# Low parts of the first eight weight tiles to VectorE, the causal mask's cast to ScalarE

## The chip, the cores and the metric

The kernel runs on one NeuronCore of one Trainium2 chip. The metric is the device time of one execution in microseconds (us); the time before is the median of three runs. The engines are called by the profile's names: PE (TensorE's matmuls), PEld (its weight loads), DVE (VectorE), ACT (ScalarE), POOL (GpSimd) and SP (SyncE, which issues the weight transfers).

## What is computed

Two layers of a decoder trunk on 256 tokens of width 1024, batch 1, in float32. Each layer normalises its input, multiplies it with one combined projection, sends the columns through two attention groups and a final projection, and adds a squared-ReLU MLP. Cut to the part that matters here:

```python
for l in range(DEPTH):                       # DEPTH = 2
    h = _rms_norm(x, attn_norm[l])
    proj = h @ w_in[l]                       # 1024 -> 1720 columns
    (q_a, k_c, v_c, k_s, v_s, k_w, v_w, g_a, c_q, c_kv, k_r) = jnp.split(proj, offsets, axis=-1)
    ...                                      # sparse attention o_a and latent attention o_b, both causal
    x = x + mixed @ w_out[l]
    h = _rms_norm(x, mlp_norm[l])
    x = x + jnp.square(jax.nn.relu(h @ w_ff1[l])) @ w_ff2[l]
return _rms_norm(x, final_norm)
```

## The kernel before

**Products in three passes.** A dense product is done as three matmuls on numbers split into a high part (rounded to the type fp32r) and a low part (the rest): high times high (line 352), high activation times low weight (353), low activation times high weight (354), in `mm3`. Every weight tile is therefore split after it has landed.

**The weight stream.** `PLAN` lists the weight tiles in the order in which PE uses them; `ask(n)` keeps up to `n` tiles ahead. For a tile it issues the transfer into one of six `raw` buffers on SP's queue (line 321), and, where the tile is to be split, has ACT cast it to `whi` in two halves (line 334) and DVE or POOL subtract, `wlo = raw - whi`, in two halves (line 336). There are six buffers of `whi` and `wlo`. A tile here is "tile n", the n-th entry of `PLAN`, counted from 1. In a layer tiles 1 to 4 are the block `kcs` (two chunks of 512 columns each, so a half is one chunk), 5 to 8 the block `q` (the same), 9 to 11 `kw` (280 columns a chunk, three chunks), 12 to 15 `lat` (416 columns), 16 to 18 the latent up-projections, 19 to 26 the compression weights, which are not split, and then the output projection and the MLP.

**Who subtracts.** `lo_eng()` (line 312) gives tiles 1 and 2 of the whole run and all odd tiles to DVE, even ones to POOL. `at_w[1]` is the tile's number.

**The start.** `main` loads `x` in four quarters with the gain and tile loads in between, and four `norm` chains make the normalised activations: DVE multiplies by the gain (line 425), PE transposes (line 384), ACT casts the high part (line 393) and DVE subtracts the low part (line 394). The order of the four is half 0 of token tiles 0 and 1 (`h_191` high, `h_192` low), then half 1 of both (`h_241` high, `h_242` low). PE meanwhile runs `proj_both` for block `kcs` of layer 0: pairs of chunks, token tile 0 and then token tile 1 for each pair; chunks 4 to 7 (tiles 3 and 4) need half 1. After it PE runs block `q` from tile 5. `kcs_after` rotates the results on DVE (lines 446, 449, 451, 455) and copies the others on ACT (line 868).

**The mask.** `main` casts the causal mask from the constants `cs` into `maskb` (line 1171); `mask_for` multiplies it into the attention scores (line 652).

**What sets the order.** PE's and SP's orders are written by `Driver`, a list scheduler with ranks and estimated times that runs when the kernel is built. DVE, ACT and POOL are ordered by the framework's own scheduler at build time, each engine then executing strictly in that order; `urgent()` raises the priority of a few instructions, among them lines 393, 394 and 425.

Of the kernel before, what the change touches and what calls it, by code (L numbers as in the profile page):

```python
# [17 lines left out]
L = 2  # L18
# [87 lines left out]
def _plan():  # L106
    plan = []

    def add(chunks, per, n, split=True):
        plan.extend((min(per, chunks - a), n, split) for a in range(0, chunks, per))  # L110

    for name, (_, n) in BLOCKS.items():
        add(KC, PER_TILE[name], n)
    add(1, 1, 1024)
    add(2, 1, 768)
    add(16, 2, 512, False)
    add(16, 2, 512)
    for q in range(NQ):
        add(32, 2, 512)
    return plan  # L120


PLAN = _plan() * L
# [103 lines left out]
def trunk(ctx: ExitStack, tc: tile.TileContext, x, wst, gains, pos, cw2, cst, out):  # L227
    nc = tc.nc
# [28 lines left out]
    def load_x(t, nb):  # L257
        n = slice(nb * 512, nb * 512 + 512)
        nc.sync.dma_start(X[t][:, n], x[t * P : (t + 1) * P, n])
# [19 lines left out]
    def K(name):  # L279
        a, n = CST[name]  # L280
        return cs[:, a : a + n]
# [4 lines left out]
    maskb = const.tile([P, P], BF16, name="maskb")  # L286
# [7 lines left out]
    def warm_up(n):  # L294
        if n:
            o = PS("s")
        for _ in range(n):
            mm(o, zero, zero[:, None, :].to_broadcast([P, 4, P]), start=True, stop=True)
# [9 lines left out]
    at_w = [0, 0]  # L308
    queue = []

    def lo_eng():
        return "v" if at_w[1] <= 2 or at_w[1] % (len(PLAN) // L) % 2 == 1 else "g"

    def ask(n):

        while at_w[1] < len(PLAN) and len(queue) < n:
            k, cols, split = PLAN[at_w[1]]
            at_w[1] += 1
            m = k * cols
            r = raw_p.tile([P, 1024], F32, name="raw")  # L320
            nc.sync.dma_start(r[:, :m], wst[at_w[0] : at_w[0] + P * m].rearrange("(p n) -> p n", p=P))
            at_w[0] += P * m
            part = lambda a: [a[:, c * cols : (c + 1) * cols] for c in range(k)]
            if split:
                hi = wp.tile([P, 1024], F32R, name="whi")
                lo = wp.tile([P, 1024], F32R, name="wlo")
                eng = lo_eng()

                def cuts(n):
                    step = m // n  # L330
                    return [slice(a, a + step) for a in range(0, m, step)]

                for v in cuts(2):
                    nc.scalar.copy(hi[:, v], r[:, v])  # L334
                for v in cuts({"v": 2, "g": 2}[eng]):
                    E(eng).tensor_sub(lo[:, v], r[:, v], hi[:, v].bitcast(F32))  # L336
                queue.append(list(zip(part(hi), part(lo))))
            else:
                queue.append(part(r))

    def weights(chunks):

        while chunks:
            ask(1 + 4)
            got = queue.pop(0)
            chunks -= len(got)
            yield from got
# [62 lines left out]
    def after_x(t, a, n):  # L410

        ss = sumsq(X[t][:, a : a + n], n)
        r = sm.tile([P, 1], F32, name="mean", bufs=6)
        nc.gpsimd.tensor_scalar(r, ss, 1.0 / D, EPS if a == 0 else mean[t], op0=OP.mult, op1=OP.add)
        mean[t] = r
# [42 lines left out]
    def layer(l, hT):  # L458
# [487 lines left out]
        for ch, r in enumerate(weights(16)):  # L946
            for j in range(4):
                a, hf = divmod(j, 2)
                mm(  # L949
                    hid[32 * j : 32 * j + 32, :],  # L950
                    FT[:, a, ch].rearrange("p g b -> p (g b)"),
                    r[:, a * 256 + hf * 128 : a * 256 + hf * 128 + 128],
                    start=ch == 0,
                    stop=ch == 15,
                    tile_position=(0, 32 * j),
                )
            yield "pe", 300, 0
        dr.spawn(1, hidden_chain(hid))


# [158 lines left out]
    def begin(l, halves=()):  # L1119

        g = gain(l, "attn", halves)
        h = [None, None]
        if l == L:
            for t in range(NT):
                dr.spawn(0, finish(t, g))
        else:
            for nb in range(2):
                for t in range(NT):
                    dr.spawn(0, norm(t, nb, g, h, (l, "attn")))
        return h  # L1130
# [16 lines left out]
    def main():  # L1147
        def load_a():
            nc.sync.dma_start(idt, cst[:, :P])
            load_x(1, 0)  # L1150
            ask(2)

        def load_b():
            load_x(1, 1)
            ask(5)

        def next_x():
            load_a()
            load_x(0, 1)

        load_x(0, 0)
        h = begin(0, (next_x, load_b))
        for t in range(NT):
            for nb in range(2):
                dr.event(("x", t, (0, "attn"), nb * 512), [2000, 5000, 2600, 5500][2 * t + nb])
        for nb in range(2):
            for t in range(NT):
                after_x(t, nb * 512, 512)
        nc.sync.dma_start(cs, cst)
        nc.vector.tensor_copy(identb, ident)  # L1170
        nc.vector.tensor_copy(maskb, K("causal"))
        yield "event", ("h", 0, (0, "attn"), 0)
        warm_up(4)
        for l in range(L):
            h = yield from layer(l, h)

    dr.spawn(9, main())
    with tc.manual_schedule(engines={mybir.EngineType.PE, mybir.EngineType.SP}):
        dr.run()
# [19 lines left out]
```

## Time and profile before

| | |
|---|---|
| median of three runs | 642.43 us |
| the three runs | 642.43, 645.75, 640.5 us |
| the profiled execution, own time | 646.11 us |
| its span, first to last instruction | 644.3 us |
| PE busy / DVE / ACT / POOL | 621.4 / 420.4 / 354.6 / 300.4 us |
| mean granted clock of PE | 0.986 of full |

The profile is one execution of its own and lies above all three runs shown. Times in the rows are microseconds from the start of the span, and in a row of the timeline the first number is the start, the second the busy time of the merged instructions, "x4" their count, and the bracket the idle time of that engine just before with what ended it. Ends of matmuls are modelled; starts are what to compare.

### The profile page before, as it was taken

The page shows a single profiled execution, that of the slowest core. Times are in us where ns is not written, and L with a number is a line of the kernel's source. Part 1 is how long each engine was busy: PE and PEld are TensorE (multiplying, and loading weights), DVE is VectorE, ACT ScalarE, POOL GpSimd, SP SyncE. Part 2 cuts the span into 40 slices and gives each one's busy share as a digit, 9 for nine tenths or more (in the row PEclk, how much of TensorE's full clock was granted, in tenths as well). Part 3 has the DMA queues.
Part 4 walks back from the last instruction along what each step waited for, and adds up shares of the span by engine and source line. Part 5 has one row for each costly group of instructions (what it writes and reads, how often), then busy time and mean ns, then how long its engine had stood idle before and what let it go on. Part 6 is the DMA issues. An engine that isn't in the chain of part 4 may idle for free.

```text
span 644.3 us, 10909 instructions
## 1 busy us (share of the span) xinstructions
PE 621.4 (96%) x4099; PEld 548.3 (85%) x4099; DVE 420.4 (65%) x665; ACT 354.6 (55%) x735; POOL 300.4 (47%) x298
## 2 busy tenths in 40 slices
PE   7899899999999999999999889999999999999995
PEld 4697688889889899899888768798998998998985
DVE  4797778675656647558677866866664673764662
ACT  5566667565535546355564475765663654554551
POOL 2675404344553645445466631244544554554351
PEclk8899999999999999999999898999999999999998
DMA  8756733155555655745644665114547565565601
GB/s 306 264 175 206 236 116 100 34 198 173 185 169 191 208 182 166 226 155 186 213 126 134 211 212 199 34 66 149 177 142 220 164 200 174 193 204 176 198 1 66
DMA packets 31732, 108.48 MB, mean 168 GB/s; under 512 B 3776, under 2 KB 4416, under 8 KB 31680
## 3 DMA queue, kind: packets, MB, share of 16 engines
q1 hardware_dynamic: 31392, 107.27, 50.8%
q8 instruction: 32, 0.52, 0.3%
q10 hardware_dynamic: 288, 0.52, 0.2%
q14 instruction: 20, 0.16, 0.1%
HBM read 106.73 MB, written 1.05 MB: 167 GB/s over the span
## 4 chain that ended last, share of the span: by engine, by line
PE 85%; DVE 7%; ACT 4%; DMA 3%; issue 1%; SPq 0%; POOL 0%; POOLq 0%; ACTq 0%
PE acc L352 24%; PE acc L354 24%; PE acc L353 24%; PE tr L384 4%; DVE wlo L336 2%; PE pv L708 2%; DMA raw<-in_wst_dram 2%; PE pv L759 2%; ACT whi L334 1%; PE acc L949 1%; PE s L693 1%; DMA x<-in_x_dram 1%; PE s L746 1%; ACT p L646 1%; DVE qmT L233 1%
## 5 line engine op out<-in xcount | busy, mean ns | idle before, releaser
L336 POOL TENSOR_TENSOR wlo<-raw,whi 128x512 fp32r<-128x512 f32 (+3 forms) x178 | 245.0, 1397 | 221.2 <-ACT whi L334 220.9
L334 ACT CAST whi<-raw 128x512 fp32r<-128x512 f32 (+2 forms) x360 | 201.4, 610 | 113.6 <-PE acc L354 74.7
L336 DVE TENSOR_TENSOR wlo<-raw,whi 128x512 fp32r<-128x512 f32 (+3 forms) x182 | 170.5, 973 | 58.4 <-ACT whi L334 58.3
L352 PE MATMUL acc<-h,whi 128*128 128x256 f32 x512 | 145.3, 284 | 0.0
L354 PE MATMUL acc<-h,wlo 128*128 128x256 f32 x512 | 145.0, 283 | 0.0
L353 PE MATMUL acc<-h,whi 128*128 128x256 f32 x512 | 145.0, 283 | 0.0
L352 PE MATMUL acc<-whi,u 128*128 128x512 f32 (+1 forms) x264 | 101.5, 384 | 0.0
L353 PE MATMUL acc<-wlo,u 128*128 128x512 f32 (+1 forms) x264 | 101.2, 383 | 0.0
L354 PE MATMUL acc<-whi,u 128*128 128x512 f32 (+1 forms) x264 | 101.1, 383 | 0.0
L352 PEld LDWEIGHTS acc<-h,whi 128*128 128x128 f32 x512 | 98.3, 192 | 0.2
L353 PEld LDWEIGHTS acc<-h,whi 128*128 128x128 f32 x512 | 98.3, 192 | 0.2
L354 PEld LDWEIGHTS acc<-h,wlo 128*128 128x128 f32 x512 | 98.3, 192 | 0.0
L1057 DVE TENSOR_TENSOR sq<-relu 128x512 f32<-128x512 f32 x32 | 37.2, 1161 | 38.9 <-ACT relu L1053 38.9
L354 PEld LDWEIGHTS acc<-whi,u 128*128 128x128 f32 x264 | 49.6, 188 | 9.8
L353 PEld LDWEIGHTS acc<-wlo,u 128*128 128x128 f32 x264 | 49.7, 188 | 9.4
L352 PEld LDWEIGHTS acc<-whi,u 128*128 128x128 f32 x264 | 49.7, 188 | 9.3
L1029 DVE SCALAR_TENSOR_TENSOR x<-acc,r,x 128x512 f32<-128x512 f32 (+1 forms) x33 | 24.1, 731 | 49.0 <-PE acc L354 49.0
L1053 ACT ACTIVATE relu<-acc 128x512 f32<-128x512 f32 x32 | 19.0, 594 | 59.3 <-PE acc L354 59.3
L352 PE MATMUL acc<-whi,h 128*128 128x512 f32 (+2 forms) x112 | 41.2, 368 | 0.0
L353 PE MATMUL acc<-wlo,h 128*128 128x512 f32 (+2 forms) x112 | 40.2, 359 | 0.2 <-POOL wlo L336 0.2
L354 PE MATMUL acc<-whi,h 128*128 128x512 f32 (+2 forms) x112 | 39.9, 357 | 0.0
L646 ACT ACTIVATE p<-s,nm 128x128 f32<-128x128 f32 (+1 forms) x96 | 33.9, 430 | 7.9 <-DVE nm L640 4.0
(185 smaller groups left out, 913.3 us busy)
## 6 DMA issues: line engine op xcount, KB each, us to landing
raw<-in_wst_dram SPq DMA_DIRECT2D x178, 512.0 KB, 4.2
raw<-in_wst_dram SPq DMA_DIRECT2D x8, 416.0 KB, 3.3
raw<-in_wst_dram SPq DMA_DIRECT2D x4, 420.0 KB, 3.3
raw<-in_wst_dram SPq DMA_DIRECT2D x4, 384.0 KB, 3.1
x<-in_x_dram SPq DMA_DIRECT2D x4, 256.0 KB, 6.3
g_mix<-in_gains_dram SPq DMA_DIRECT2D x2, 512.0 KB, 5.8
g_mlp<-in_gains_dram SPq DMA_DIRECT2D x2, 512.0 KB, 5.1
g_attn<-in_gains_dram SPq DMA_DIRECT2D x2, 512.0 KB, 3.9
```

The lines of the kernel that those rows point to most:

```text
L334: nc.scalar.copy(hi[:, v], r[:, v])
L336: E(eng).tensor_sub(lo[:, v], r[:, v], hi[:, v].bitcast(F32))
L352: mm(acc, ah, wh, start=start, stop=False, **k)
L353: mm(acc, ah, wl, start=False, stop=False, **k)
L354: mm(acc, al, wh, start=False, stop=stop, **k)
L384: nc.tensor.transpose(tr[:rows, c, :], col, ident)
L646: nc.scalar.activation(p[:, k], s[:, k], AF.Exp, bias=nm[:, a : a + 1], scale=scale)
L708: mm(o[:, a, br, :], pts[a // per][:, ((a % per) * 2 + br) * nk + kt, :], V[:, kt, br, g, :], start=kt == 0, stop=kt == nk - 1)
L759: mm(o[:, r, :], pts[r // per][:, (r % per) * nk + kt, :], VM[:, kt, hb * 4 + r, :], start=kt == 0, stop=kt == nk - 1)
L1029: nc.vector.scalar_tensor_tensor(X[t][:, c], acc, scale, X[t][:, c], op0=OP.mult, op1=OP.add)
L1053: nc.scalar.activation(r, acc, AF.Relu)
L1057: nc.vector.tensor_mul(sq, r, r)
```

## The change

The subtraction `wlo = raw - whi` of tiles 4, 6 and 8 of layer 0 goes from POOL to DVE (tiles 1, 2, 3, 5 and 7 were there already). The cast of the mask goes from DVE to ACT. A statement without effect (`if True:`) shifts the line numbers behind it by one. Layer 1 is left as it is, since the tile number runs on.

```diff
     def lo_eng():
-        return "v" if at_w[1] <= 2 or at_w[1] % (len(PLAN) // L) % 2 == 1 else "g"
+        return "v" if at_w[1] <= 8 or at_w[1] % (len(PLAN) // L) % 2 == 1 else "g"
@@
-            yield "pe", 300, 0
+            if True:
+                yield "pe", 300, 0
@@
         nc.vector.tensor_copy(identb, ident)
-        nc.vector.tensor_copy(maskb, K("causal"))
+        nc.scalar.copy(maskb, K("causal"))
```

The framework orders DVE, ACT and POOL anew. On DVE, at the point in layer 0 where the low parts of half 1 are made (`h_242`, first for token tile 0, then for token tile 1) and block `kcs` of token tile 0 is rotated:

```order
 L394 TENSOR_TENSOR h_242<-tr,h_241 128x4x128
-L336 TENSOR_TENSOR wlo<-raw,whi 128x512 x2
-L1171 CAST maskb<-cs 128x128
+L336 TENSOR_TENSOR wlo<-raw,whi 128x512 x4
 L394 TENSOR_TENSOR h_242<-tr,h_241 128x4x128
-L336 TENSOR_TENSOR wlo<-raw,whi 128x512
+L336 TENSOR_TENSOR wlo<-raw,whi 128x512 x3
 L446 SCALAR_TENSOR_TENSOR ra<-s,rx,cs 128x128
 L449 SCALAR_TENSOR_TENSOR rb<-s,rx,cs 128x2x32 x2
 L336 TENSOR_TENSOR wlo<-raw,whi 128x512
+L451 TENSOR_TENSOR kd<-ra,rb 128x256
+L336 TENSOR_TENSOR wlo<-raw,whi 128x512
```

Between the two `h_242` there stand four halves (tiles 4 and 5) where two halves (tile 5) and the mask stood; behind the second there are three halves (tile 6 and the first of tile 7) where there was one, and the last three halves of tiles 7 and 8 lie between the rotations.

On POOL, behind the row scales of both token tiles, before its first halves of block `kw`:

```order
 L863 TENSOR_TENSOR rx<-mean,mhalf 128x1
 L864 TENSOR_SCALAR rx<-rx 128x1
-L336 TENSOR_TENSOR wlo<-raw,whi 128x512 x6
 L336 TENSOR_TENSOR wlo<-raw,whi 128x420 x2
 L336 TENSOR_TENSOR wlo<-raw,whi 128x416 x2
```

The six halves of tiles 4, 6 and 8 are gone; POOL's next work is tile 10.

On ACT, at the high part of half 1 of token tile 1 (the second `h_241`):

```order
 L334 CAST whi<-raw 128x512 x4
 L393 CAST h_241<-tr 128x4x128
+L1172 CAST maskb<-cs 128x128
 L334 CAST whi<-raw 128x512 x6
+L334 CAST whi<-raw 128x420 x2
```

The mask stands directly behind the high part of half 1 and ahead of the casts of tiles 6, 7 and 8; the cast of tile 9 has moved ahead of the copies of line 868. The orders of PE and SP are the same in both kernels.

## Rows read from the trace of the kernel before

**Rows 1.** The page, its head and part 1: busy us, share, count.

```profile
span 644.3 us, 10909 instructions
...
PE 621.4 (96%) x4099; PEld 548.3 (85%) x4099; DVE 420.4 (65%) x665; ACT 354.6 (55%) x735; POOL 300.4 (47%) x298
```

**Rows 2.** Stretches: length; busy PE, PEld, DVE, ACT, POOL; clock; DMA share; GB/s.

```profile
40.00:60.00 20.00, 18.73 (x123) 17.45 (x122) 18.03 (x36) 11.72 (x32) 16.73 (x25) 1.00 0.60 188
...
125.00:200.00 75.00, 75.00 (x477) 68.02 (x476) 45.73 (x60) 41.04 (x76) 36.23 (x30) 1.00 0.55 179
```

**Rows 3.** Who PE waited for, whole run: us in total, times, longest.

```profile
PE s L354 <- DVE h L394: 2.7, 1, 2.7
...
PE tr L384 <- DVE qT L530: 1.3, 1, 1.3
```

**Rows 4.** The chain that ended last, in time: start, us, what.

```profile
20.82 1.28 DVE maskb L1171
22.10 0.61 DVE h L394
...
63.12 5.27 DMA raw<-in_wst_dram
```

**Rows 5.** PE in order of time, around the wait for the last low part.

```profile
19.71 0.40 PE L353 MATMUL s<-wlo,h 128*128 128x512 f32 x1
22.76 0.80 PE L354 MATMUL s<-whi,h 128*128 128x512 f32 x1 [2.65 <-DVE h L394]
...
25.84 0.39 PE L352 MATMUL s<-whi,h 128*128 128x512 f32 x1
...
27.90 0.39 PE L352 MATMUL acc<-whi,h 128*128 128x512 f32 x1
```

**Rows 6.** DVE in order of time, 6 to 27 us.

```profile
6.55 0.22 DVE L1170 CAST identb<-idt 128x128 bf16<-128x128 f32 x1
...
10.35 2.49 DVE L336 TENSOR_TENSOR wlo<-raw,whi 128x512 fp32r<-128x512 f32 x4
...
16.79 0.69 DVE L394 TENSOR_TENSOR h<-tr,h 128x512 fp32r<-128x512 f32 x1 [1.41 <-ACT h L393]
18.34 2.55 DVE L336 TENSOR_TENSOR wlo<-raw,whi 128x512 fp32r<-128x512 f32 x2 [0.86 <-ACT whi L334]
...
22.02 0.68 DVE L394 TENSOR_TENSOR h<-tr,h 128x512 fp32r<-128x512 f32 x1
...
26.81 0.35 DVE L446 SCALAR_TENSOR_TENSOR ra<-s,rx,cs 128x128 f32<-128x128 f32 x1 [3.01 <-PE s L354]
```

**Rows 7.** DVE in order of time, window 19.5 to 19.9 alone.

```profile
19.12 1.77 DVE L336 TENSOR_TENSOR wlo<-raw,whi 128x512 fp32r<-128x512 f32 x1
```

**Rows 8.** POOL in order of time, its low parts up to tile 10.

```profile
17.36 8.82 POOL L336 TENSOR_TENSOR wlo<-raw,whi 128x512 fp32r<-128x512 f32 x6 [0.88 <-ACT whi L334]
31.25 2.49 POOL L336 TENSOR_TENSOR wlo<-raw,whi 128x420 fp32r<-128x420 f32 x2 [5.08 <-ACT whi L334]
```

**Rows 9.** ACT in order of time, 16 to 30 us.

```profile
16.65 2.18 ACT L334 CAST whi<-raw 128x512 fp32r<-128x512 f32 x4
18.73 0.58 ACT L393 CAST h<-tr 128x512 fp32r<-128x512 f32 x1
19.21 3.22 ACT L334 CAST whi<-raw 128x512 fp32r<-128x512 f32 x6
...
29.50 0.36 ACT L868 ACTIVATE V<-s,rx 128x128 f32<-128x128 f32 x1
```

**Rows 10.** Short stretches, columns as in rows 2.

```profile
22.70:25.50 2.80, 2.74 (x7) 2.17 (x8) 1.10 (x1) 0.00 (x0) 2.80 (x3) 0.50 0.96 340
```

**Rows 11.** The same view, the stretch with POOL at rest.

```profile
9.00:12.70 3.70, 3.70 (x11) 1.97 (x10) 3.48 (x6) 3.55 (x8) 0.12 (x1) 0.58 1.04 407
```

**Rows 12.** The constants' transfer: its issue on SP, us from issue to landing.

```profile
8.82 0.33 SPq L1169 DMA_DIRECT2D cs<-in_cst_dram  x1
...
DMA to landing us min/median/max: 8.4/8.4/8.4
```

## The prediction

> **What bounds the kernel now.** I read the page's head first: PE is busy for 621.4 of 644.3 us [rows 1], so a change can only pay where PE stands still, some 23 us in all. The busy time by stretch shows that from 125 us on PE has no idle time at all for long pieces (75.00 of 75.00 us) [rows 2]: whatever PE gains or loses before that is not made up there, and passes to the end. The list of PE's waits then says where it stands still: its longest single wait is 2.7 us, for the subtraction of line 394 on DVE [rows 3]. The same place stands in the chain of work that ended last, and there the mask's cast (1.28 us) and the subtraction (0.61 us) are links of it [rows 4]. So the change works where time is to be had.
>
> The timeline shows how that wait comes about. PE starts its last matmul of the running set at 19.71, has no work from about 20.11, and goes on at 22.76, when the low part of half 1 of token tile 1 is there [rows 5]. DVE started that subtraction at 22.02, although ACT had its high part ready at 18.73 + 0.58 = 19.31 [rows 6, 9]. What stood ahead of it on DVE were the two halves of tile 5, from 18.34 on, and the mask. The second half alone ran 1.77 us [rows 7], the mask 1.28 us [rows 4]. The same subtraction with POOL at rest took 2.49 / 4 = 0.62 us in a run of four [rows 6], and the cast of `identb`, a tile of the same size, 0.22 us [rows 6]. POOL's six halves run from 17.36 on, 8.82 / 6 = 1.47 us each [rows 8]. I read the stretched DVE rows as these two engines in each other's way. Transfers are not the reason: at 9.00 to 12.70, where the run of four took 0.62 us each, they moved 407 GB/s [rows 11]. Line 394 itself, which takes one operand from PSUM, ran 0.68 us beside POOL's work and 0.69 us before it [rows 6].
>
> PE also loses time behind the wait. From 22.70 to 25.50 the granted clock was 0.50, the 1.2 GHz level [rows 10], after those 2.65 us without work. From 22.76 to 27.90 PE started 16 matmuls, 5.14 us; the last nine, at full clock, took 27.90 - 25.84 = 2.06 us, 0.229 each [rows 5]. Sixteen at that pace are 3.66 us, so 1.48 us went to the low clock and the refilling of the pipeline.
>
> **The change part by part.**
>
> Removed from POOL: six halves, 8.82 us [rows 8]. None of it was waited for by PE here; its worth is that DVE runs alone. POOL's next work (tile 10) starts at 31.25, after 5.08 us of idleness [rows 8], so nothing comes earlier because of it.
>
> Added ahead of the critical subtraction on DVE: two halves (tile 4). Removed from there: the mask. I take 0.62 us a half, the price of the run with POOL at rest [rows 6], because POOL has no other work in that stretch. The bounds are 0.60, that run's start-to-start distance ((2.49 - 0.69) / 3), and 1.77 us, the dearest half of the trace here [rows 7]. DVE ends the first `h_242` at 16.79 + 0.69 = 17.48 [rows 6]. ACT's casts of tiles 4 and 5 run from 16.65 for 2.18 us, so the four are there at about 17.2, 17.8, 18.3 and 18.8 [rows 9]; DVE, taking them at 17.5, 18.1, 18.7 and 19.3, waits for none. They end at about 19.98. The high part is there (19.31), so line 394 runs to 19.98 + 0.68 = 20.66, and PE goes on 0.06 later as now (22.76 against 22.02 + 0.68), at 20.72. That is **2.0 us earlier** than 22.76, with 0.6 us of the wait left. It cannot start before 19.31 + 0.68 + 0.06 = 20.05, when PE has still work: the most is the whole wait, 2.65 us.
>
> The clock: after a wait of 1.27 us at 53.78 (the 1.3 us for line 530 [rows 3]) the stretch from 40 to 60 us keeps clock 1.00 [rows 2]. A wait of 0.6 us should keep it too, so I count **1.4 us** of the 1.48. The bounds are 0 and 1.48.
>
> The mask on ACT: its nearest row is a 128x128 activation, 0.36 us [rows 9]; 0.22, `identb` on DVE, is the lower end. It stands behind the high part of half 1, so it can't delay that. Its constants were issued at 8.82 and landed 8.4 us later, at 17.2 [rows 12], so it does not wait. It pushes back ACT's casts of tiles 6 to 8 (from 19.21 [rows 9]) by 0.4 us at most. PE reaches tile 6 after 16 matmuls of `kcs` and 6 of tile 5, at about 20.7 + 22 x 0.229 = 25.7, five microseconds behind the cast. Cost: nothing.
>
> Moved behind the critical place: the halves of tiles 6 and 8 now also stand on DVE, and the last three of tiles 7 and 8 stand among the rotations, which wait for PE's results. The worst of them is the last half of tile 8. With PE at 20.72, `kcs` of token tile 0 is done ten matmuls later, about 23.1; then DVE has two rotations of three rows (0.65 us each, 26.81 to the next half before [rows 6]), one addition and three halves, 23.1 + 1.3 + 0.4 + 1.9 = 26.7. PE needs that half for its eighth chunk of `q`, 16 + 21 matmuls behind 20.72, at 29.2. It has 2.5 us to spare. Cost: nothing; with each of these three halves at 1.77 it would be 3.4 us more and a wait of 0.9.
>
> Sum: 2.0 + 1.4 = **3.4 us**, against the profile's own time 646.11 - 3.4 = 642.7. That execution lies 3.7 us over the median of the runs, 642.43, so I carry the difference over: 642.4 - 3.4 = **639.0 us**. The ends of the known costs: 2.65 + 1.48 = 4.1 us gained (638.3), and 2.0 without the clock's share (640.4).
>
> The Trainium skill warns of such a move: its page "Perfetto Trace Analysis", section "Optimizing Scalar/DVE Operations", says that VectorE and GpSimd share a read port of the SBUF, so that shifting work between the two might not help. By it the sum would be near nothing. The rows bear out the sharing, but here the half on POOL costs 1.47 us and the half on DVE alone 0.62.
>
> **The rivals.**
>
> *The wait shrinks, the clock's part does not come* (2.0 us, 640.4). Either the clock falls all the same, or it did not fall in the runs that make the median, which would fit their being shorter than the profile. Against it stands the 1.27 us wait without a fall.
>
> *Given back later* (0 us, 642.4). Between 40 and 60 us DVE is busy 18.03 and POOL 16.73 of 20 us [rows 2], and PE waits there for DVE's line 530 [rows 3]; if what ends these waits does not move with PE, the gain ends there. The warning quoted from the Trainium skill's page comes out here as well. For this rival speaks how full that stretch is, and the 5.27 us transfer in the chain at 63.12 [rows 4]. Against it: the chain leads through these places, and that transfer starts when PE gives a `raw` buffer free, so both move with PE.
>
> *More than counted* (5 to 7 us, about 636). The later collisions of DVE and POOL fall differently and one of the waits of 1 to 3 us goes too. Nothing in the order aims at it.
>
> *Slower: four halves ahead of the critical subtraction instead of two.* If DVE is slow there for another reason than POOL, four at 1.77 us run from 17.48 to 24.56, line 394 ends at 25.24 and PE goes on at 25.3, 2.5 us later than now: 645.0. It decides from (22.02 - 17.48) / 4 = 1.13 us a half. Against it stands the run of four at 0.62 with transfers at full rate.
>
> **How the numbers follow.** Forecast (2.8 to 4.1 us gained) 0.55; without the clock 0.16; given back 0.16; more 0.08; slower 0.05. About 1%, 6.4 us, is what a measurement of this kernel can tell from no change. The three runs before lie from -1.9 to +3.3 us about their median, and this spread goes on top of the cases. The low end is 635.5 (the 638.3 of the bound, less a spread of 2.8), the high end 644.5 (nothing gained, and 2 more). Faster by over 1% means under 636.0: the fourth case and the edge of the spread, 0.10. Slower means over 648.9: even the slower rival gives only 645.0, so 0.04. Within 1%: 0.86.
>
> **What would show it.** In the changed profile DVE has four halves of about 0.62 us between the two `h_242`, the second `h_242` ends near 20.7, PE's wait there is under 1 us, the granted clock from 20 to 28 us is 1.00, and PE starts its first matmul into `acc` near 24.5 instead of 27.90. At 60 and at 125 us PE stands 3 to 4 us earlier than before. POOL has nothing from 17 us to tile 10. I am wrong if the halves run over 1.1 us with POOL at rest, if a wait for line 336 appears in block `q`, or if the 3.4 us are there at 28 us and gone by 80.

## The result, and the profile after

The changed kernel takes 639.71 us (median of 20 runs, 635.54 to 644.65) against 643.4 us (median of 20 runs, 639.24 to 648.15). The ratio of the two means is 0.9936, 95% interval 0.9909 to 0.9963: 4.1 us less, between 2.4 and 5.9 (the medians differ by 3.7). That is within 1%, as forecast, and clear of no change. The forecast was 639.0 with a range of 635.5 to 644.5.

The page's head and part 1 of the changed kernel:

```profile
span 636.6 us, 10910 instructions
...
PE 618.1 (97%) x4099; PEld 546.2 (86%) x4099; DVE 420.0 (66%) x670; ACT 354.6 (56%) x736; POOL 291.9 (46%) x292
```

Against [rows 1] the span is 7.7 us shorter, nearly twice what the medians say; where the other half comes from is told under the third heading. POOL lost 8.5 us of work, and DVE, which took it over, is no busier (420.0 against 420.4): its own instructions became as much shorter as it got more of them.

DVE in order of time (start, busy us, instruction, count, idle time before and its cause), the part that answers to [rows 6]:

```profile
16.12 0.69 DVE L394 TENSOR_TENSOR h<-tr,h 128x512 fp32r<-128x512 f32 x1
16.73 2.49 DVE L336 TENSOR_TENSOR wlo<-raw,whi 128x512 fp32r<-128x512 f32 x4
19.14 0.68 DVE L394 TENSOR_TENSOR h<-tr,h 128x512 fp32r<-128x512 f32 x1
19.91 2.05 DVE L336 TENSOR_TENSOR wlo<-raw,whi 128x512 fp32r<-128x512 f32 x3
...
25.39 0.68 DVE L336 TENSOR_TENSOR wlo<-raw,whi 128x512 fp32r<-128x512 f32 x1
```

Four halves now run in 2.49 us, 0.62 each, where two had taken 2.55; the second low part of `h` follows at once. The last row is the last half of tile 8, behind the first rotations.

ACT and POOL at the same place, which answer to [rows 9] and [rows 8]:

```profile
18.07 0.58 ACT L393 CAST h<-tr 128x512 fp32r<-128x512 f32 x1
18.55 0.31 ACT L1172 CAST maskb<-cs 128x128 bf16<-128x128 f32 x1
19.26 1.14 ACT L334 CAST whi<-raw 128x512 fp32r<-128x512 f32 x2 [0.41 <-DMA raw<-in_wst_dram]
```

```profile
15.92 0.22 POOL L864 TENSOR_SCALAR rx<-rx 128x1 f32<-128x1 f32 x1
26.73 2.49 POOL L336 TENSOR_TENSOR wlo<-raw,whi 128x420 fp32r<-128x420 f32 x2 [10.59 <-ACT whi L334]
```

The mask costs ACT 0.31 us, and behind it ACT still waits 0.41 us for a transfer, so the cast is hidden. POOL rests for 10.6 us.

PE around the wait ([rows 5]), and the stretch from 20 to 28 us (length; busy PE, PEld, DVE, ACT, POOL; granted clock; share and GB/s of the transfers):

```profile
19.05 0.40 PE L353 MATMUL s<-wlo,h 128*128 128x512 f32 x1
19.88 0.50 PE L354 MATMUL s<-whi,h 128*128 128x512 f32 x1 [0.43 <-DVE h L394]
...
23.65 0.39 PE L352 MATMUL acc<-whi,h 128*128 128x512 f32 x1
```

```profile
20.00:28.00 8.00, 8.00 (x36) 6.59 (x37) 7.34 (x18) 5.17 (x11) 1.27 (x2) 1.00 0.86 305
```

The wait is 0.43 us instead of 2.65, the clock stays at full, and PE works the whole stretch.

The two traces of the changed kernel reach the first `h_242` subtraction 1.9 us apart (16.12 and 18.00 us). So the runs below are compared by distances inside a trace: **A**, from DVE's start of the first `h_242` subtraction to PE's first matmul into `acc`; **B**, from there to PE's first multiplication with the mask (the line of `mask_for`). In us:

| kernel | first `h_242` | into `acc` | first mask | A | B | PE's wait | ratio to before (95%) |
|---|---|---|---|---|---|---|---|
| before | 16.79 | 27.90 | 58.05 | 11.11 | 30.15 | 2.65 | |
| changed | 16.12 | 23.65 | 53.13 | 7.53 | 29.48 | 0.43 | 0.9936 (0.9909 to 0.9963) |
| changed, again | 18.00 | 25.54 | 55.00 | 7.54 | 29.46 | 0.44 | 0.9951 (0.9914 to 0.9987) |
| tiles only | 17.27 | 24.96 | 54.43 | 7.69 | 29.47 | 0.57 | 0.9960 (0.9927 to 0.9993) |
| mask only | 16.27 | 24.80 | 56.32 | 8.53 | 31.52 | 1.45 | 0.9979 (0.9944 to 1.0014) |
| tile 4 and mask | 16.72 | 24.24 | 55.95 | 7.52 | 31.71 | 0.44 | 0.9979 (0.9949 to 1.0008) |
| tiles 6, 8 and mask | 16.13 | 24.66 | 55.90 | 8.53 | 31.24 | 1.45 | 0.9945 (0.9909 to 0.9980) |
| POOL loaded again | 16.25 | 29.93 | 59.40 | 13.68 | 29.47 | 4.80 | 1.0027 (0.9986 to 1.0068) |
| before, wait filled | 18.19 | 27.94 | 58.07 | 9.75 | 30.13 | 0.93 | 1.0009 (0.9969 to 1.0049) |
| tiles 1 to 18, both layers | 16.65 | 24.16 | 54.03 | 7.51 | 29.87 | 0.43 | 0.9900 (0.9865 to 0.9935) |
| the same, on another chip | 17.34 | 24.85 | 54.70 | 7.51 | 29.85 | 0.43 | 0.9841 (0.9795 to 0.9886) |
| changed, and tiles 1 to 18 of layer 1 | 15.93 | 23.44 | 52.90 | 7.51 | 29.46 | 0.43 | 0.9846 (0.9790 to 0.9903) |
| all tiles | 16.00 | 23.51 | 53.37 | 7.51 | 29.86 | 0.43 | 1.0016 (0.9977 to 1.0056) |

Each ratio is to runs of the kernel before on the same chip. Of the other versions only "tiles 6, 8 and mask", "POOL loaded again" and "tiles 1 to 18, both layers" ran beside the changed kernel itself (0.9951). The ratios tell a few us only; the distances repeat to 0.02 us in the two traces of the changed kernel.

### The profile page after: what moved, and what is told of

Same layout as the page of the kernel before. It is cut to its first block, busy times and chain, and to the rows that moved or that the text cites. A ratio compares the mean times of both kernels' runs of the same rounds, so it can differ in the third digit from the quotient of the medians.

```text
span 636.6 us, 10910 instructions
## 1 busy us (share of the span) xinstructions
PE 618.1 (97%) x4099; PEld 546.2 (86%) x4099; DVE 420.0 (66%) x670; ACT 354.6 (56%) x736; POOL 291.9 (46%) x292
## 4 chain that ended last, share of the span: by engine, by line
PE 87%; DVE 6%; ACT 3%; DMA 2%; issue 1%; SPq 0%; POOLq 0%; POOL 0%; ACTq 0%
PE acc L352 25%; PE acc L353 25%; PE acc L354 24%; PE tr L384 4%; PE pv L708 2%; DVE wlo L336 2%; DMA raw<-in_wst_dram 2%; PE pv L759 2%; PE acc L949 1%; PE s L693 1%; ACT whi L334 1%; PE s L746 1%; DMA x<-in_x_dram 1%; ACT p L646 1%; DVE qmT L233 1%
## 5 line engine op out<-in xcount | busy, mean ns | idle before, releaser
L336 POOL TENSOR_TENSOR wlo<-raw,whi 128x512 fp32r<-128x512 f32 (+3 forms) x172 | 236.6, 1396 | 225.1 <-ACT whi L334 224.8
L336 DVE TENSOR_TENSOR wlo<-raw,whi 128x512 fp32r<-128x512 f32 (+3 forms) x188 | 173.2, 958 | 56.7 <-ACT whi L334 55.9
```

## The experiments

**The tiles alone.** `lo_eng` as changed, the mask left on DVE:

```diff
-        return "v" if at_w[1] <= 2 or at_w[1] % (len(PLAN) // L) % 2 == 1 else "g"
+        return "v" if at_w[1] <= 8 or at_w[1] % (len(PLAN) // L) % 2 == 1 else "g"
```

> Only the subtractions of tiles 4, 6 and 8 go to DVE; the mask's cast stays on DVE, between the four halves and the second h_242. Theory (DVE and POOL in each other's way; the mask was dear only because of POOL): the four halves take 0.62 us each, the mask about 0.22 us instead of 1.28, the second h_242 starts some 0.2 us later than in the changed kernel, PE waits 0.6 to 0.7 us instead of 2.65, the clock stays at full, and nearly the whole gain is here: 3.2 to 3.7 us against the kernel before. Rival (the mask was the cause, its place ahead of h_242): the mask still takes about 1.3 us, PE's wait stays above 1.5 us, the gain is under 2 us.

DVE in this run:

```profile
17.88 2.49 DVE L336 TENSOR_TENSOR wlo<-raw,whi 128x512 fp32r<-128x512 f32 x4
20.28 0.22 DVE L1171 CAST maskb<-cs 128x128 bf16<-128x128 f32 x1
20.42 0.69 DVE L394 TENSOR_TENSOR h<-tr,h 128x512 fp32r<-128x512 f32 x1
```

The mask at the same place on the same engine takes 0.22 us instead of 1.28, with POOL at rest. A is 7.69, 0.16 over the changed kernel, and B is the same. So moving the mask is worth 0.16 us on top of moving the tiles, and in the trace the theory holds. The time is 2.6 us under that of before (0.5 to 4.7), an interval that covers the rival's "under 2 us" as well.

**The mask alone.** The other half:

```diff
-        nc.vector.tensor_copy(maskb, K("causal"))
+        nc.scalar.copy(maskb, K("causal"))
```

> Only the mask goes to ACT; tiles 4, 6 and 8 stay on POOL. Theory (collision of DVE and POOL): the two halves of tile 5 stay at 0.8 and 1.8 us, the second h_242 starts about 1.2 us earlier than in the kernel before (20.8 on its time axis instead of 22.0), PE's wait falls from 2.65 to about 1.4 us; gain 1.2 us, and up to 2.6 us if the clock no longer falls. Rival (the mask was the cause): the wait is under 0.7 us and the gain 3.4 us or more.

```profile
17.83 2.55 DVE L336 TENSOR_TENSOR wlo<-raw,whi 128x512 fp32r<-128x512 f32 x2 [0.87 <-ACT whi L334]
20.30 0.68 DVE L394 TENSOR_TENSOR h<-tr,h 128x512 fp32r<-128x512 f32 x1
```

The two halves of tile 5 still take 2.55 us beside POOL, and PE waits 1.45 us, as the theory had it. A shrinks by 2.58 us, at the upper end of the expectation: the wait by 1.20, and the clock did not fall. But B grows by 1.37 us, and the measured gain, 1.4 us, can't be told from none. Taken with the run before, the two halves of the change aren't additive: either one alone takes the mask's 1.06 us of collision away.

**Tile 4 and the mask, tiles 6 and 8 left on POOL.**

```diff
-        return "v" if at_w[1] <= 2 or at_w[1] % (len(PLAN) // L) % 2 == 1 else "g"
+        return "v" if at_w[1] <= 4 or at_w[1] % (len(PLAN) // L) % 2 == 1 else "g"
```

> The changed kernel, but tiles 6 and 8 stay on POOL; only tile 4 and the mask are moved. Theory (what counts is POOL at rest while DVE does the four halves ahead of the second h_242): DVE is as fast there as in the changed kernel, PE's wait is 0.4 to 0.7 us, the gain against the kernel before is the same 3.0 to 4.0 us within its interval. Rival (moving all three tiles is needed, since tile 6 on POOL starts in time to collide): the second h_242 ends over 0.7 us later than in the changed kernel and over 0.7 us of the gain is missing.

A is 7.52: for the wait itself tile 4 and the mask are all that is needed, and the rival falls. But the theory's "same gain" falls too. B is 31.71, 2.2 us over that of the changed kernel, and the time is only 1.4 us under that of before (an interval from 3.3 us less to 0.5 more). DVE, POOL and PE where it goes:

```profile
34.08 2.56 DVE L336 TENSOR_TENSOR wlo<-raw,whi 128x280 fp32r<-128x280 f32 x2
36.56 0.74 DVE L496 TENSOR_TENSOR kT<-tr,kT 128x256 fp32r<-128x256 f32 x2
```

```profile
33.73 2.59 POOL L336 TENSOR_TENSOR wlo<-raw,whi 128x416 fp32r<-128x416 f32 x2 [2.16 <-ACT whi L334]
```

```profile
37.02 0.44 PE L384 MATMUL tr<-idt,kcv 128*128 128x128 f32 x2 [1.72 <-DVE kT L496]
...
51.70 0.44 PE L384 MATMUL tr<-idt,kd 128*128 128x128 f32 x2 [1.10 <-DVE qT L530]
```

PE is 3.6 us ahead, and POOL starts tile 12 as much earlier (33.73 against 37.39 in the kernel before), but DVE comes to tile 11 only 2.17 us earlier (34.08 against 36.25). So DVE's halves of tile 11 now meet POOL's halves of tile 12: 2.56 us for 280 columns a half, where the changed kernel needs 0.80. The subtraction of line 496 behind them is late, and PE waits 1.72 us for it, then 1.10 us for line 530. With the mask alone it is the same (the two halves of tile 11 take 2.57 us there). In the changed kernel DVE's order is another here: tile 11 stands ahead of the last row (line 455) of the first rotation of `q`.

```profile
32.53 0.80 DVE L336 TENSOR_TENSOR wlo<-raw,whi 128x280 fp32r<-128x280 f32 x2
33.25 1.59 DVE L455 TENSOR_TENSOR qr<-ra,rb 128x512 f32<-128x512 f32 x1
```

The two engines meet there too, and line 455 takes 1.59 us where it took 0.69 in the kernel before, but neither wait of PE is there. So with tile 4 and the mask alone 1.56 of the 3.59 us won in A were given back in B, by a new meeting of the same two engines 10 us later.

**Tiles 6 and 8 and the mask, tile 4 left on POOL.**

```diff
-        return "v" if at_w[1] <= 2 or at_w[1] % (len(PLAN) // L) % 2 == 1 else "g"
+        return "v" if at_w[1] <= 2 or at_w[1] in (6, 8) or at_w[1] % (len(PLAN) // L) % 2 == 1 else "g"
```

> The changed kernel, but tile 4 stays on POOL; tiles 6 and 8 and the mask are moved. Theory (what counts is POOL at rest ahead of the second h_242): POOL does tile 4 beside DVE's tile 5, whose halves stay at 0.8 to 1.8 us, the second h_242 ends as with the mask alone, PE's wait is about 1.4 us and the gain 1.2 to 2.6 us. Rival (any three tiles off POOL do it): gain as in the changed kernel, wait under 0.7 us.

```profile
17.68 2.55 DVE L336 TENSOR_TENSOR wlo<-raw,whi 128x512 fp32r<-128x512 f32 x2 [0.86 <-ACT whi L334]
20.16 0.68 DVE L394 TENSOR_TENSOR h<-tr,h 128x512 fp32r<-128x512 f32 x1
```

In the trace the theory holds: wait 1.45 us, A 8.53 as with the mask alone. The measured gain is 3.5 us (1.3 to 5.9), and this interval covers both the theory's 1.2 to 2.6 and the rival's full gain. By its time the run decides nothing; its trace does.

B tells something else. Tile 11 stands early on DVE here as in the changed kernel, and the wait for line 496 is not there; yet B is 31.24, 1.76 us over the changed kernel, with two other waits of PE:

```profile
34.16 0.44 PE L384 MATMUL tr<-idt,kd 128*128 128x128 f32 x2 [0.70 <-ACT kcT L501]
...
51.65 0.44 PE L384 MATMUL tr<-idt,kd 128*128 128x128 f32 x2 [1.30 <-DVE qT L530]
```

A low B (29.5 to 29.9) came only where DVE makes the low parts of tiles 4, 6 and 8 all three. Why it takes all three stays open.

**POOL loaded again.** The changed kernel, with POOL doing the subtractions of tiles 4, 6 and 8 a second time into a tile that nobody reads:

```diff
+                if at_w[1] in (4, 6, 8):
+                    for v in cuts(2):
+                        nc.gpsimd.tensor_sub(dummy[:, v], r[:, v], hi[:, v].bitcast(F32))
```

> The changed kernel with POOL doing the subtractions of tiles 4, 6 and 8 as well, into a tile that nobody reads: DVE's, ACT's and PE's orders are those of the changed kernel, only POOL is busy again from about 16.5 us on (six halves of some 1.4 us). Theory (collision): DVE's four halves ahead of the second h_242 go from 0.62 to 1.1 us or more each, the second h_242 ends 2 us or more later than in the changed kernel, PE's wait is 2 us or more again, and the time is that of the kernel before or up to 2 us worse, at least 2.5 us over the changed kernel. Rival (it was DVE's order and the mask that mattered, not POOL at work beside it): the halves stay at 0.62 us and the gain of the changed kernel stays within 0.7 us.

DVE and POOL, and the end of PE's wait:

```profile
16.86 6.85 DVE L337 TENSOR_TENSOR wlo<-raw,whi 128x512 fp32r<-128x512 f32 x4
23.63 0.68 DVE L398 TENSOR_TENSOR h<-tr,h 128x512 fp32r<-128x512 f32 x1
```

```profile
16.82 9.70 POOL L340 TENSOR_TENSOR dummy<-raw,whi 128x512 f32<-128x512 f32 x6 [0.19 <-ACT whi L335]
```

```profile
24.36 0.80 PE L358 MATMUL s<-whi,h 128*128 128x512 f32 x1 [4.80 <-DVE h L398]
```

This is the run that settles the cause of the wait. Order and data of DVE are those of the changed kernel; only POOL works beside it. The four halves go from 2.49 to 6.85 us, 1.71 each, and POOL's own take 1.62 each (1.47 in the kernel before). PE waits 4.80 us, A is 2.57 us longer than in the kernel before, and the time is 4.9 us over that of the changed kernel beside which it ran (1.0027 against 0.9951 of 644.14). It is the slower rival of the prediction in its place and near its price (it gave 2.5 us more); what it lacked in the changed kernel is POOL.

**The kernel before, its wait filled.** Eight matmuls on zeros in PE's queue ahead of the matmul that waits:

```diff
-    def mm3(acc, a, w, start, stop, **k):
+    def mm3(acc, a, w, start, stop, fill=0, **k):
...
         mm(acc, ah, wl, start=False, stop=False, **k)
+        warm_up(fill)
...
-                        mm3(accs[t], h(c + i), wc, c + i == 0, c + i == chunks - 1)
+                        mm3(accs[t], h(c + i), wc, c + i == 0, c + i == chunks - 1, fill=8 if t == 1 and c + i == 4 else 0)
```

> The kernel before with eight matmuls on zeros (128x512, bf16, some 0.22 us each at full clock) put into PE's queue right ahead of the matmul that waits; they add to the work and leave out none. Theory (1.4 us of the gain is the clock that falls after the wait): the wait for the second h_242 ends at the same time, the granted clock behind it stays at full, PE reaches its first matmul into acc 1.0 to 1.5 us earlier than in the kernel before, and so does the end. Rival (the clock is not part of it): no difference beyond 0.3 us, or 0.5 us slower for the added matmuls.

```profile
21.35 1.90 PE L298 MATMUL s<-zero 128*128 128x512 bf16 x8
24.17 0.50 PE L355 MATMUL s<-whi,h 128*128 128x512 f32 x1 [0.93 <-DVE h L395]
...
27.94 0.39 PE L352 MATMUL acc<-whi,h 128*128 128x512 f32 x1
```

```profile
20.00:28.00 8.00, 7.06 (x31) 4.45 (x30) 7.96 (x10) 4.86 (x10) 8.00 (x6) 1.00 0.72 243
```

DVE ends at the same distance as before (its second `h_242` starts 5.25 us after the first, against 22.02 - 16.79 = 5.23), yet A is 9.75 instead of 11.11: 1.36 us come from the stretch behind the wait, where the clock did not fall this time. B is unchanged. In these two traces, then, the clock's term of the sum is real and of the size that was given. The time shows nothing of it: 1.0009, from 2.0 us less to 3.2 us more. Whether the clock falls behind this wait in every execution of the kernel before, and whether the filling is what kept it up, stays open: behind another wait, of 2.3 us, it fell in one trace of the changed kernel and not in the other (the rows are under the next heading).

**More tiles on DVE.** First the tiles 1 to 18 of both layers, all that PE uses ahead of the compression weights:

```diff
-        return "v" if at_w[1] <= 2 or at_w[1] % (len(PLAN) // L) % 2 == 1 else "g"
+        n = (at_w[1] - 1) % (len(PLAN) // L) + 1
+        return "v" if n <= 18 or n % 2 == 1 else "g"
```

> A wider version: the subtractions of the first 18 tiles (all those ahead of the compression weights) of both layers go to DVE, the mask to ACT. Theory (each half beside POOL's work costs DVE more than doing POOL's half too): in the stretch from 25 to 55 us and its like in layer 1 DVE's halves run 0.5 to 0.62 us, and PE's waits for DVE there (2.3 us in layer 1 for line 496) shrink; 1 to 3 us under the changed kernel. Rival (DVE is the fuller engine there, 18 of 20 us busy): DVE falls behind, PE waits longer for it, same or slower than the changed kernel by up to 3 us.

It takes 0.9900 of the time before (0.9865 to 0.9935), 6.4 us less; the changed kernel took 0.9951 beside it. Run again on another chip, with the two versions that follow, it takes 0.9841 (0.9795 to 0.9886).

> The version with the first 18 tiles of both layers on DVE once more, beside the other two on one chip: about 1% under the kernel before.

To find where that lies, the changed kernel with the first 18 tiles of layer 1 alone:

```diff
-        return "v" if at_w[1] <= 8 or at_w[1] % (len(PLAN) // L) % 2 == 1 else "g"
+        l1 = 98 < at_w[1] <= 116
+        return "v" if at_w[1] <= 8 or l1 or at_w[1] % (len(PLAN) // L) % 2 == 1 else "g"
```

> The changed kernel with the first 18 tiles of layer 1 on DVE as well; tiles 9 to 18 of layer 0 stay as in the changed kernel. Theory (the extra of the wider version lies in layer 1, where PE's wait of 2.3 us for line 496 and the fall of the clock behind it went): 2 to 3 us under the changed kernel, as the wider version, wait under 0.8 us at 350 us. Rival (the extra lies in layer 0's tiles 9 to 18): no more than 0.7 us under the changed kernel.

It takes 0.9846 (0.9790 to 0.9903) on the chip where the wider version took 0.9841. Six runs of each leave some 4 us open, and the changed kernel did not run beside them, so the times alone do not place the extra. The traces do: the tiles 9 to 18 of layer 0 add nothing ahead of the first mask, where B is 29.85 to 29.87 with them and 29.46 without, and the difference shows in layer 1. There PE's waits between 340 and 365 us and DVE's rows of line 336 are, first in the changed kernel, then in the version with 18 tiles in both layers (line numbers shifted by one):

```profile
PE tr L384 <- DVE kT L496: 2.3, 1, 2.3
```

```profile
349.61 2.23 DVE L336 TENSOR_TENSOR wlo<-raw,whi 128x416 fp32r<-128x416 f32 x2
...
354.02 3.19 DVE L336 TENSOR_TENSOR wlo<-raw,whi 128x384 fp32r<-128x384 f32 x2
```

```profile
PE tr L385 <- DVE kT L497: 0.5, 1, 0.5
```

```profile
351.09 1.09 DVE L337 TENSOR_TENSOR wlo<-raw,whi 128x416 fp32r<-128x416 f32 x2
...
355.11 0.55 DVE L337 TENSOR_TENSOR wlo<-raw,whi 128x384 fp32r<-128x384 f32 x1
```

A half of 416 columns falls from 1.1 to 0.55 us, one of 384 from 1.6 to 0.55, and 1.8 us of PE's wait go. The version with layer 1's tiles alone has the same wait of 0.5 us.

Last, the whole stream on DVE:

```diff
-        return "v" if at_w[1] <= 2 or at_w[1] % (len(PLAN) // L) % 2 == 1 else "g"
+        return "v"
```

> All subtractions of the run on DVE, none on POOL; the mask on ACT. DVE then has 360 halves of about 0.62 us, some 220 us, beside about 245 us of other work, so about 70% of the span. Theory (outside the attention stages PE has no idle time, so there is nothing to win there): the same as the version with the first 18 tiles within 2 us. Rival (DVE becomes the bound in the MLP, where it also has lines 1057, 1058 and 1029): waits of PE for DVE appear between 125 and 345 us and the time is over that of the changed kernel.

The time is 1.0016 of that of before (0.9977 to 1.0056): the whole gain is gone, and both theories miss the place. Between 125 and 345 us PE stays full, so DVE is not the bound in the MLP. The stretches from 60 to 125 and 365 to 440 us, with their attention, are worse (first this version, then the one with layer 1's 18 tiles; columns as above):

```profile
60.00:125.00 65.00, 59.78 (x480) 51.15 (x475) 47.75 (x118) 40.91 (x99) 12.16 (x20) 1.00 0.34 111
...
365.00:440.00 75.00, 69.72 (x582) 58.41 (x581) 55.14 (x134) 47.48 (x119) 13.02 (x22) 1.00 0.38 123
```

```profile
60.00:125.00 65.00, 63.06 (x493) 54.32 (x491) 46.27 (x115) 42.33 (x102) 22.80 (x28) 1.00 0.38 126
...
365.00:440.00 75.00, 73.32 (x550) 62.50 (x548) 53.87 (x124) 48.19 (x114) 28.32 (x33) 1.00 0.42 139
```

PE works 3.3 and 3.6 us less there; its longest waits, up to 2.5 us, are for line 722, in front of which DVE has taken halves of the output projection's weights, which PE needs only after the attention:

```profile
67.73 0.68 DVE L336 TENSOR_TENSOR wlo<-raw,whi 128x512 fp32r<-128x512 f32 x1
...
68.94 0.41 DVE L722 TENSOR_TENSOR otmp<-pv,wv 128x256 f32<-128x256 f32 x1
```

```profile
69.49 1.97 PE L708 MATMUL pv<-V,pt 128*128 128x65 f32 x16 [2.44 <-DVE otmp L722]
```

That explains some 7 of the 8.7 us between the spans of these two traces (639.0 and 630.3). The execution in the trace is the quickest of that version's twelve (640.81 us, median 648.47), so what the others lose beyond it is not seen and stays open.

## Why the prediction was right, point by point

**What bounds the kernel**: right. PE was idle from 20.1 to 22.8 us, and the gain passed through the long stretch without idle time: PE is 4.92 us ahead at the first mask (53.13 against 58.05) and 5.09 at the first mask of layer 1 (364.29 against 369.38). That the two agree so closely is in part luck: in the second trace of the changed kernel the way between these masks is 308.97 us, against 311.16 and, before, 311.33. It had no fall of the clock on that way (the rows are below), and in layer 0 a wait of 0.49 us for line 722 where the two others had 1.76 and 1.79.

**The halves at 0.62 us with POOL at rest**: right to the second digit (2.49 us for four). The collision was read from rows in which an instruction was slow beside POOL and its like was quick without; the run with POOL loaded again shows it as a cause.

**The wait**: 0.6 us left were forecast, 0.43 measured. The change of A, 11.11 - 7.53 = 3.58 us, stands against a sum of 3.4; 2.22 of it is the wait, where the prediction had 2.0, and the filled wait puts 1.36 on the clock, where it had 1.4. That is the account of single traces. With the 0.67 us of B below they give 4.25 us, and 2.89 without the clock's part; the interval of the measured gain, 2.4 to 5.9 us, covers both, so the times do not show that part.

**The mask on ACT at no cost**: right, 0.31 us between rows that wait for transfers. Its share of the gain is 0.16 us; the prediction did not separate it.

**The halves moved behind, at no cost**: right in the sum, too simple in the working. The last half of tile 8 ended at 25.39 + 0.68 = 26.07, 6.19 us after PE went on (19.88), where 26.7 - 20.72 = 5.98 was forecast. But the step looked only at what PE needs in block `q`. It did not ask what DVE and POOL meet next once PE is early, and with tiles 6 and 8 left on POOL, B was 2.2 us longer than in the changed kernel.

**What was not forecast**: 0.67 us in B. PE's wait of 1.27 us for line 530 [rows 3] is not there any more; no row here says where the other 0.6 us of it went. The prediction had the changes of these waits as rivals, one with a gain and one with a loss, and took none as likely; the runs with parts of the change show both signs, 29.47 to 31.71 in B against 30.15 before.

**From the profile to the median**: the prediction carried its 3.4 us over to the median of three runs, 642.43, and came to 639.0. The median of 20 runs before is 643.4; from there the same sum gives 640.0. The measured 639.71 lies between the two, so the spread of three runs weighed as much in the forecast time as what the sum had left out. The difference of the two profiles would have misled. Their spans differ by 7.7 us, of which A and B are 4.25. Another 0.67 lies ahead of A, in the start. And 7.7 - 5.09 = 2.6 come after the first mask of layer 1 (369.38 before, 364.29 changed), where the change moves nothing. Of these, 1.54 us lie behind a wait of 1.79 us for line 722 that both traces have: from line 708 behind it (385.76 and 379.86) to line 579 (404.04 and 396.60) it is 18.28 us before and 16.74 in the changed kernel. The clock fell there in the one and not in the other. First the kernel before, with an earlier fall behind PE's wait of 2.29 us for line 496, then the changed kernel, whose fall behind the same wait (2.27 us) lies ahead of its first mask:

```profile
363.00:369.00 6.00, 5.44 (x21) 5.28 (x22) 4.56 (x10) 3.18 (x9) 3.05 (x4) 0.72 0.55 180
388.00:390.00 2.00, 2.00 (x9) 0.83 (x12) 1.71 (x4) 0.74 (x2) 0.46 (x1) 0.50 0.06 23
```

```profile
359.00:362.00 3.00, 3.00 (x10) 2.87 (x10) 1.89 (x6) 2.17 (x8) 1.55 (x3) 0.52 0.81 280
380.00:390.00 10.00, 10.00 (x107) 8.29 (x108) 5.89 (x17) 6.54 (x18) 1.98 (x5) 1.00 0.80 259
```

In the second trace of the changed kernel the wait for line 496 is as long (2.30 us, up to 359.71), and the clock stays at full behind it:

```profile
360.00:363.00 3.00, 3.00 (x18) 2.97 (x17) 1.89 (x6) 2.25 (x8) 1.36 (x3) 1.00 0.87 306
```

So such falls come and go between executions of one program. Over the 20 runs of the changed kernel the mean clock goes from 0.997 (635.66 us) to 0.981 (644.65), and the time rises as it falls; how much of the spread it causes is not shown. One profile against one profile would have told 7.7 us for a change worth 4.

## What to carry to other kernels

Where VectorE and GpSimd share a stream of work, price an instruction by whether the other engine works beside it: a half moved off GpSimd can make VectorE quicker although it has more to do. Do it where TensorE waits for VectorE, and only there; the same move over the whole run put unneeded weights ahead of attention work and lost the whole gain. And after a stall is gone, look for the next place where the two engines meet, because the shift in time alone can bring them together.

The best versions here are the changed kernel with the first 18 tiles of layer 1 on VectorE too, or the first 18 of both layers: 0.9846 and 0.9841 of the time before, on one chip. Where the second of them ran beside the change itself, it took 0.9900 against 0.9951.

## What the runs showed of the hardware

VectorE's subtraction of two operands in SBUF (128x512) takes 0.62 us in a run with GpSimd at rest, 1.28 us on average beside it in the kernel before, and 1.71 us beside an unbroken run of GpSimd subtractions, whose own take 1.62 us: the two engines then go on at one pace, about one instruction each in 1.7 us. The cast of the mask, with one operand, goes from 0.22 to 1.28 us. The subtraction with one operand in PSUM stays at 0.68 to 0.69 us in every run. The Trainium skill, page "SBUF — State Buffer", section "Who interferes with whom", has it so: a VectorE instruction with two SBUF inputs contends with a GpSimd instruction that reads SBUF, a cast can do so in a two-port mode, and the engine that comes second waits for the whole instruction of the other. The rows agree in kind, with the prices just given; that the mask's cast ran in a two-port mode no run here shows.

At the start of the kernel TensorE's clock fell to the 1.2 GHz level behind the wait of 2.65 us and behind that of 4.80 us, and not behind waits of 0.43, 0.57, 0.93 and 1.45 us. But the length of the wait alone does not decide. Behind the 2.3 us for line 496 it fell in one trace of the changed kernel and not in the other, and with all tiles on VectorE it stayed at full behind a wait of 2.44 us for line 722:

```profile
69.00:75.00 6.00, 5.02 (x56) 4.17 (x57) 3.38 (x9) 3.74 (x10) 0.91 (x2) 1.00 0.92 324
```
